# One-hots for the later gathers of a routed-expert layer, made one chunk earlier

## The chip, the cores and the metric

The kernel runs on one core of a Trainium2 chip. The metric is the device time of one execution in microseconds (us), lower is better. In what follows TensorE (PE in the profile) multiplies matrices, with its weight loads shown apart (PEld); VectorE is DVE, ScalarE is ACT, and SyncE (SP) issues every transfer from memory.

## The reference

Two layers of a decoder trunk over 256 tokens of 1024 features in float32: two mixers, a dense feed-forward block, and at the end a routed one. Only that last block is touched:

```python
def moe_swiglu(h, router, w_gate, w_up, w_down):
    t = h.reshape(b * s, d)
    logits = (t @ router).astype(jnp.float32)
    top_val, top_idx = lax.top_k(logits, TOP_K)          # 2 of 8 experts
    top_w = jax.nn.softmax(top_val, axis=-1)
    gates = ...                                          # zero where an expert is not chosen
    out = jnp.zeros_like(t)
    for e in range(N_EXPERTS):
        out = out + gates[:, e:e + 1] * swiglu(t, w_gate[e], w_up[e], w_down[e])
    return out.reshape(b, s, d)
```

Each expert has a gate and an up matrix of 1024 x 2816 and a down matrix of 2816 x 1024.

## The kernel before

The kernel computes for each expert only the rows (tokens) that chose it. The experts are sorted by their number of rows. The four largest ("large", ranks 0 to 3) get 128 rows each and are computed with split weights: every weight is the sum of a rounded part `wh` and a rest `wl`, and three products replace one. The four others ("small") get 64 rows and use the weights as they are. An expert's rows are fetched on TensorE: a one-hot matrix (128 tokens by 128 places, 1 where a token sits in that place) is multiplied with the normalised activations `xnh` and `xnl`. The function `one_hots` makes it on VectorE with one `tensor_tensor` for each half of the tokens, comparing `iota` with the tokens' places `poso`; `gather_all(j, oh, dst)` is the product for the j-th block of 128 features, and ScalarE copies its result into `dst`.

Weights come in units of 1 MB, three to a chunk of 256 hidden features: two for gate and up (`gu0`, `gu1`) and one for down (`dn`). An expert has 11 chunks (FC). Units are loaded in the order of their use into a ring of places (`raw` five times, `xres`, `xg1`, `more`, `fl`, `wx`, `wy`); a place is loaded anew once its unit is split (large) or multiplied (small). The splits run on ScalarE (`wh`) and VectorE (`wl`), two half units each, and are issued by `st.ahead`.

From the first expert's chunk on the order of the work is written out by hand: a list `steps`, and every engine works through its instructions in that order. The large experts' chunks are numbered g = 0 to 43 (expert p, chunk c, g = 11 p + c); the small ones follow LAG = 4 chunks later. From g = 5 on the steps of one g are: transposes of the previous large chunk (`tr`), `gu0`, late scatters, transposes of the small chunk, `dn` of the previous large chunk, `gu1` with the activation and two splits, `rest`, and then the small expert's `dn`, `gu0`, `gu1`.

The step `rest` holds what is not part of the chunk pipeline: the transposed one-hots for the scatters (`oht_of`), and the gathers. At g = 0 to 3 the small experts' rows are gathered, at g = 6 to 9 those of the large experts 1 and 2 together, two blocks of features in each chunk, and at g = 13 to 16 (p = 1, c = 2 to 5) those of expert 3. The one-hots of a group are made at its first gather. They lie in a tile of the ring `tw`, which has 12 buffers and also holds the hidden activations and their transposes.

Of the kernel before, what the change touches and what calls it, by code (L numbers as in the profile page):

```python
# [19 lines left out]
P = 128  # L20
# [35 lines left out]
LAG = 4  # L56
# [338 lines left out]
def kernel(ctx: ExitStack, tc: tile.TileContext, a, out: bass.AP):  # L395
# [29 lines left out]
    def tw(n=512, np_=P, dt=F32):  # L425
        return rec.tile(wkp, [P, 512], dt, "tw", TW, name="tw")[:np_, :n]

    def pa():
        return rec.tile(psp, [P, 512], F32, "ps", 8, name="ps")
# [104 lines left out]
    def bc(ap, shape):  # L534
        return ap.to_broadcast(shape)
# [237 lines left out]
    def ff_gu(st, xs, gu, u, ahead=True):  # L773
        wh, wl = st.next(ahead)
        for b in range(len(xs)):
            for kk in range(4):
                k = 4 * u + kk
                mm3(gu[b], xs[b][0][:, k, :], xs[b][1][:, k, :], wh[:, kk * 512:(kk + 1) * 512],
                    wl[:, kk * 512:(kk + 1) * 512], k == 0, k == 7)

    def ff_act(gu, scales=None, act=None):
        hs = []
        for b in range(len(gu)):
            si = tw(256)
            hh = tw(256)
            if scales:
                tact(si, gu[b][:, 0:256], AF.Silu, scale=scales[b])
                V.scalar_tensor_tensor(hh, gu[b][:, 256:512], scales[b], si, op0=OP.mult, op1=OP.mult)
            else:
                (act or tact)(si, gu[b][:, 0:256], AF.Silu)  # L790
                V.tensor_tensor(hh, gu[b][:, 256:512], si, OP.mult)
            hs.append(hh)
        return hs

    def ff_tr(hs):
        n = 2 * len(hs) * P
        tp = pa()
        transposes([h[:, i * P:(i + 1) * P] for i in range(2) for h in hs], tp)
        th, tl = tw(n, dt=F32R), tw(n, dt=F32R)
        S.activation(th, tp[:, :n], AF.Copy)  # L800
        V.tensor_tensor(tl, tp[:, :n], th.bitcast(F32), OP.subtract)
        return th, tl
# [277 lines left out]
    mo = scope("m")  # L1080
# [389 lines left out]
    def one_hots(lo, n, width=P):  # L1470

        t = tw(2 * n * width, dt=F32R).rearrange("p (b e s) -> p b e s", b=2, e=n)
        for b in range(2):
            V.tensor_tensor(t[:, b], bc(iota[:, None, 0:width], [P, n, width]),
                            bc(poso[:, b, lo:lo + n, None], [P, n, width]), OP.is_equal)
        return t

    def both_halves(r):

        t = tw(256, dt=F32R).rearrange("p (b s) -> p b s", b=2)  # L1480
        for b in range(2):
            V.tensor_scalar(t[:, b].rearrange("p (i s) -> p i s", i=2), bc(iota[:, None, 0:HALFP], [P, 2, HALFP]),
                            poso[:, b, r:r + 1], None, op0=OP.is_equal)
        return t
# [6 lines left out]
    def gather(k, ohs, n):  # L1491

        o = pa()[:, 0:n]
        for i, src in enumerate((xnh, xnl)):
            for b in range(2):
                mmx(o, src[:, b, k * P:(k + 1) * P], ohs(b), i + b == 0, i + b == 2)
        return o, k2("gf1k", k, k + 1)
# [5 lines left out]
    def gather_all(k, oh, dst):  # L1503

        n, w = oh.shape[2], oh.shape[3]
        o, gain = gather(k, lambda b: oh[:, b].rearrange("p e s -> p (e s)"), n * w)
        S.activation(dst[:, :, k], o.rearrange("p (e s) -> p e s", e=n), AF.Copy, scale=gain)
# [8 lines left out]
    def y_split(yps):  # L1516
        rec.late = 0
        y = [(tw(dt=F32R), tw(dt=F32R)) for i in range(2)]
        for i in range(2):
            rec.late = HALF if i else 0  # L1520
            S.activation(y[i][0], yps[i], AF.Copy)
            V.tensor_tensor(y[i][1], yps[i], y[i][0].bitcast(F32), OP.subtract)
        return y

    def scatter(t, y, g, acc, store=False):
        for i in range(2):
            rec.late = HALF if i else 0
            cs = slice(i * 512, (i + 1) * 512)
            for b in range(2):
                sp = pa()  # L1530
                T.matmul(sp, t[:, b * P:(b + 1) * P], y[i][0], start=True, stop=False)
                T.matmul(sp, t[:, b * P:(b + 1) * P], y[i][1], start=False, stop=True)
                V.scalar_tensor_tensor(acc[:, b, cs], sp, g(b), acc[:, b, cs], op0=OP.mult, op1=OP.add)
                if store:
                    dma(ov[:, b, cs], acc[:, b, cs])
        rec.late = 0
# [5 lines left out]
    def large_split(src):  # L1542
        x = large_tile()
        S.activation(x[0], src, AF.Copy)
        V.tensor_tensor(x[1], src, x[0].bitcast(F32), OP.subtract)
        return x


    def sm_gu(xs, gu, u):
        w = st.next(False)  # L1550
        for kk in range(4):
            k = 4 * u + kk
            wv = w[:, kk * 512:(kk + 1) * 512].rearrange("p (g f) -> p g f", g=2)
            for i in range(2):
                mmx(gu[i * HALFP:(i + 1) * HALFP, 0:256].rearrange("p (g f) -> p g f", g=2), xs[:, k],
                    wv[:, :, i * P:(i + 1) * P], k == 0, k == 7)
        st.done()

    def sm_act(gu):
        si, hh = tw(P), tw(P)  # L1560
        tact(si, gu[:, 0:P], AF.Silu)
        V.tensor_tensor(hh, gu[:, P:256], si, OP.mult)
        return hh

    def sm_tr(hh):
        tp = pa()
        transposes([hh], tp)
        t = tw(P)
        S.activation(t, tp[:, 0:P], AF.Copy)
        return t  # L1570

    def sm_dn(t, y, first, last):
        w = st.next(False)
        for hf in range(2):
            for i in range(2):
                mmx(y[hf][i * HALFP:(i + 1) * HALFP, :], t[:, i * HALFP:(i + 1) * HALFP],
                    w[:, i * 1024 + hf * 512:i * 1024 + (hf + 1) * 512], first, last)
        st.done()
# [57 lines left out]
    for n, (k, it) in enumerate(steps):  # L1636
        if k == "late":
            while pend:
                scatter(*pend.pop(0))
            continue  # L1640
        sm, p, c = it
        if k in ("gu0", "gu1"):
            if k == "gu0":
                gu[sm] = pa()
            if sm:
                sm_gu(xs[:, p], gu[sm], unit_of[k])
            else:
                ff_gu(st, [xb], [gu[sm]], unit_of[k], False)
            if k == "gu1":
                hs[sm] = sm_act(gu[sm]) if sm else ff_act([gu[sm]])  # L1650
                if not sm and c == FC - 1 and p < BIG - 1:
                    xb = large_split(xl[:, p % 2])
                if not sm:
                    st.ahead(HL)
                    st.ahead(HL)
                if c == 0:
                    ohs[sm] = n, both_halves(BIG + p) if sm else one_hots(p, 1)[:, :, 0]
        elif k == "tr":
            ts[sm] = sm_tr(hs[sm]) if sm else ff_tr(hs[sm])
            if not sm:  # L1660
                st.ahead(HL)
        elif k == "dn":
            if c == 0:
                ys[sm] = [pa(), pa()]
            if sm:
                sm_dn(ts[sm], ys[sm], c == 0, c == FC - 1)
            else:
                ff_dn(st, ts[sm], [ys[sm]], c == 0, c == FC - 1, False)
            if c == FC - 1:
                r = p + (BIG if sm else 0)  # L1670
                pend.append((ohts[sm], y_split(ys[sm]), lambda b, r=r: gateo[:, b, r:r + 1], x3, n == len(steps) - 2))
        else:
            for e in list(ohs):
                if n >= ohs[e][0] + 5:
                    o = ohs.pop(e)[1]
                    ohts[e] = oht_of(o[:, 0], o[:, 1])
            if p == 0 and c < LAG:
                for j in range(2 * c, 2 * c + 2):
                    gather_all(j, oh_s, xs)
            if p == 0 and LAG + 2 <= c < LAG + 6:  # L1680
                if c == LAG + 2:
                    xl, oh_l = mo([P, 2, 8, P], "xg0"), one_hots(1, 2)
                for j in range(2 * (c - LAG - 2), 2 * (c - LAG - 1)):
                    gather_all(j, oh_l, xl)
            if p == 1 and 2 <= c < 6:
                if c == 2:
                    oh_l = one_hots(3, 1)
                for j in range(2 * c - 4, 2 * c - 2):
                    gather_all(j, oh_l, xl[:, 0:1])
    man.close()  # L1690
# [179 lines left out]
```

## Time and profile before

| | |
|---|---|
| runs | median 1151.38 us (1150.53 to 1153.55, 3 runs) |
| profiled execution | 1152.82 us, span 1151.0 us |
| TensorE busy | 1113.1 us, 97% |
| VectorE busy | 723.1 us, 63% |
| ScalarE busy | 601.4 us, 52% |
| mean granted TensorE clock | 0.985 |
| moved by DMA | 348.15 MB, mean 302 GB/s |

The span runs from the first to the last instruction of the profiled execution; its own time is 1.8 us longer. Busy shares are means over the whole span. Instructions recorded through a helper all carry that helper's line (L333, or L522 to L524 for the three products), so they are told apart by the tiles: `tw<-c,poso` is the making of one-hots, `ps<-tw,xnh` the first product of a gather, `ps<-cp,tw` a transpose, `wl<-raw,wh` half of a split.

### The profile page before, as it was taken

The numbers are of one execution on the slowest core, as the hardware profiler recorded it, in microseconds if no ns is written. First come the engines' busy times: TensorE is split into PE (matmuls) and PEld (weight loads), VectorE is DVE, ScalarE is ACT, GpSimd is POOL, SyncE is SP. The second block draws the span as 40 slices with busy tenths as digits, with TensorE's granted clock in tenths as the row PEclk, the third lists the DMA queues.
The fourth block names the chain that finished last, engine by engine and source line by source line (L and its number), as shares of the span: only waits on it lengthen the run. The fifth ranks groups of instructions, "written<-read, shape, count | busy, mean of one in ns | idle before, by whom it ended". The sixth has DMA issues, their size and how long they took to land.

```text
span 1151.0 us, 16659 instructions
## 1 busy us (share of the span) xinstructions
PE 1113.1 (97%) x6100; PEld 833.5 (72%) x6100; DVE 723.1 (63%) x1325; ACT 601.4 (52%) x1134; POOL 29.1 (3%) x59
## 2 busy tenths in 40 slices
PE   8999999999999999998999799999999999999997
PEld 7887888888787877875676567666666666676653
DVE  6999954544388867785356646556556556565542
ACT  5868644444378656474355435545454554544430
POOL 1050000000300000000000000000000000000000
PEclk9999999999999999899899999999999999999999
DMA  9551555556343633379799989999999999999996
GB/s 345 214 215 37 185 218 188 186 181 218 113 156 124 254 149 147 144 272 382 289 401 408 411 333 390 414 422 422 421 421 420 423 421 422 421 422 422 421 422 248
DMA packets 52216, 348.15 MB, mean 302 GB/s; under 512 B 5920, under 2 KB 6048, under 8 KB 11680
## 3 DMA queue, kind: packets, MB, share of 16 engines
q1 hardware_dynamic: 52128, 347.02, 76.0%
q8 instruction: 50, 0.82, 0.3%
q14 instruction: 38, 0.31, 0.1%
HBM read 345.95 MB, written 1.05 MB: 301 GB/s over the span
## 4 chain that ended last, share of the span: by engine, by line
PE 89%; DMA 5%; DVE 3%; ACT 2%; issue 0%; SPq 0%; DVEq 0%; ACTq 0%
PE ps L333 23%; PE ps L522 19%; PE ps L524 19%; PE ps L523 19%; PE ps L328 10%; DMA raw<-in_moe_dram 3%; DMA more<-in_moe_dram 2%; DVE wl L333 1%; ACT tw L328 1%; DMA raw<-in_w_dram 0%; DVE wl L328 0%; DVE tw L328 0%; ACT wh L333 0%; DVE xres L333 0%; ACT wh L328 0%
## 5 line engine op out<-in xcount | busy, mean ns | idle before, releaser
L333 ACT ACTIVATE tw<-ps 128x256 fp32r<-128x256 f32 (+3 forms) x202 | 72.6, 365 | 360.8 <-PE ps L524 212.5
L522 PE MATMUL ps<-wh,fh 128*128 128x512 f32 (+2 forms) x632 | 254.5, 403 | 0.0
L523 PE MATMUL ps<-wl,fh 128*128 128x512 f32 (+2 forms) x632 | 245.5, 389 | 0.0
L333 DVE TENSOR_TENSOR tw<-ps,tw 128x256 f32<-128x256 f32 (+3 forms) x158 | 64.6, 427 | 264.7 <-ACT tw L333 264.7
L333 DVE TENSOR_TENSOR wl<-raw,wh 128x1024 fp32r<-128x1024 f32 x156 | 183.7, 1224 | 55.9 <-ACT wh L333 55.4
L333 ACT ACTIVATE wh<-raw 128x1024 fp32r<-128x1024 f32 x156 | 155.2, 1050 | 43.7 <-PE ps L524 37.8
L524 PE MATMUL ps<-wh,fh 128*128 128x512 f32 x352 | 138.5, 394 | 0.0
L522 PEld LDWEIGHTS ps<-wh,fh 128*128 128x128 f32 x632 | 119.4, 189 | 22.2 <-issue 0.2
L523 PEld LDWEIGHTS ps<-wl,fh 128*128 128x128 f32 x632 | 119.4, 189 | 21.7 <-issue 0.2
L524 PE MATMUL ps<-wh,fl 128*128 128x512 f32 (+2 forms) x280 | 107.6, 384 | 0.0
L522 PE MATMUL ps<-wh,tw 128*128 128x512 f32 (+1 forms) x252 | 103.2, 410 | 1.8 <-ACT tw L333 1.1
L524 PE MATMUL ps<-wh,tw 128*128 128x512 f32 (+1 forms) x252 | 99.3, 394 | 0.0
L523 PE MATMUL ps<-wl,tw 128*128 128x512 f32 (+1 forms) x252 | 99.2, 394 | 0.0
L333 PE MATMUL ps<-raw,xs 128*64 128x256 f32 x672 | 78.4, 379 | 0.0
L524 PEld LDWEIGHTS ps<-wh,fh 128*128 128x128 f32 x352 | 66.4, 189 | 14.5
L328 DVE TENSOR_TENSOR wl<-raw,wh 128x512 fp32r<-128x512 f32 x113 | 74.7, 680 | 2.9 <-ACT wh L328 2.9
L333 PEld LDWEIGHTS ps<-raw,xs 128*64 128x64 f32 x672 | 47.9, 137 | 33.4 <-issue 11.7
L328 ACT ACTIVATE wh<-raw 128x512 fp32r<-128x512 f32 (+1 forms) x104 | 59.7, 620 | 18.7 <-PE ps L524 11.5
L524 PEld LDWEIGHTS ps<-wh,fl 128*128 128x128 f32 x280 | 52.6, 188 | 10.7 <-DVE fl L328 0.2
L522 PEld LDWEIGHTS ps<-wh,tw 128*128 128x128 f32 x252 | 47.6, 189 | 15.0 <-ACT tw L333 2.2
L524 PEld LDWEIGHTS ps<-wh,tw 128*128 128x128 f32 x252 | 47.4, 188 | 11.4 <-DVE tw L328 0.4
L523 PEld LDWEIGHTS ps<-wl,tw 128*128 128x128 f32 x252 | 47.5, 189 | 9.3
(319 smaller groups left out, 1744.2 us busy)
## 6 DMA issues: line engine op xcount, KB each, us to landing
raw<-in_moe_dram SPq DMA_DIRECT2D x120, 1024.0 KB, 13.9
raw<-in_ffn_dram SPq DMA_DIRECT2D x30, 1024.0 KB, 4.8
xg<-in_moe_dram SPq DMA_DIRECT2D x24, 1024.0 KB, 13.4
more<-in_moe_dram SPq DMA_DIRECT2D x24, 1024.0 KB, 12.9
fl<-in_moe_dram SPq DMA_DIRECT2D x24, 1024.0 KB, 13.2
raw<-in_w_dram SPq DMA_DIRECT2D x23, 1024.0 KB, 4.9
wx<-in_moe_dram SPq DMA_DIRECT2D x23, 1024.0 KB, 14.2
xres<-in_moe_dram SPq DMA_DIRECT2D x23, 1024.0 KB, 14.0
```

The costliest lines, as they stand in the source:

```text
L328: return (self.name, self.cost(fn, args, kw), lambda: real(*args, **kw))
L333: return getattr(self.eng, fn)(*args, **kw)
L522: nc.tensor.matmul(ps, xh, wh, start=start, stop=False)
L523: nc.tensor.matmul(ps, xh, wl, start=False, stop=False)
L524: nc.tensor.matmul(ps, xl, wh, start=False, stop=stop)
```

## The change

The two calls of `one_hots` are moved from the first gather of their group to the `rest` step of the chunk before it: from g = 6 to g = 5 for the large experts 1 and 2, and from g = 13 to g = 12 for expert 3. The tile `xl`, into which the gathers are copied, is still allocated at the first gather.

```diff
             if p == 0 and c < LAG:
                 for j in range(2 * c, 2 * c + 2):
                     gather_all(j, oh_s, xs)
+            if (p, c) in ((0, LAG + 1), (1, 1)):
+                oh_l = one_hots(1, 2) if p == 0 else one_hots(3, 1)
             if p == 0 and LAG + 2 <= c < LAG + 6:
                 if c == LAG + 2:
-                    xl, oh_l = mo([P, 2, 8, P], "xg0"), one_hots(1, 2)
+                    xl = mo([P, 2, 8, P], "xg0")
                 for j in range(2 * (c - LAG - 2), 2 * (c - LAG - 1)):
                     gather_all(j, oh_l, xl)
             if p == 1 and 2 <= c < 6:
-                if c == 2:
-                    oh_l = one_hots(3, 1)
                 for j in range(2 * c - 4, 2 * c - 2):
                     gather_all(j, oh_l, xl[:, 0:1])
```

## Rows read from the trace of the kernel before

**Rows 1.** The page's 40 slices of 28.8 us: granted clock, DMA share, in tenths.
```profile
PEclk9999999999999999899899999999999999999999
DMA  9551555556343633379799989999999999999996
```

**Rows 2.** Windows: length, busy us (instructions) by engine, granted clock, DMA share, GB/s.
```profile
540.00:720.00 180.00, 166.75 (x931) 116.72 (x930) 98.33 (x121) 85.01 (x130) 0.00 (x0) 0.95 0.93 374
720.00:1120.00 400.00, 396.69 (x2224) 272.58 (x2224) 233.89 (x281) 194.26 (x281) 0.00 (x0) 1.00 1.01 421
...
640.00:660.00 20.00, 16.02 (x89) 11.08 (x87) 11.29 (x14) 10.95 (x15) 0.00 (x0) 0.99 1.00 407
```

**Rows 3.** The chain that ended last, in order of time: start, us, what.
```profile
543.64 3.49 DVE wl L333 x3
547.13 0.35 DVE tw L333
...
658.56 3.48 DVE wl L333 x3
...
1051.32 18.05 DMA raw<-in_moe_dram
```

**Rows 4.** Timeline of TensorE: start, us, instruction, idle time before it and its releaser.
```profile
532.26 0.44 PE L333 MATMUL ps<-cp,tw 128*128 128x128 f32 x2
...
535.29 0.27 PE L333 MATMUL ps<-cp,tw 128*128 128x128 f32 x1
...
547.62 0.82 PE L333 MATMUL ps<-tw,xnh 128*128 128x256 f32 x2 [6.51 <-DVE tw L333]
...
557.03 0.44 PE L333 MATMUL ps<-cp,tw 128*128 128x128 f32 x2
...
572.09 0.44 PE L333 MATMUL ps<-cp,tw 128*128 128x128 f32 x2
...
647.18 0.44 PE L333 MATMUL ps<-cp,tw 128*128 128x128 f32 x2
...
650.21 0.27 PE L333 MATMUL ps<-cp,tw 128*128 128x128 f32 x1
...
662.40 0.66 PE L333 MATMUL ps<-tw,xnh 128*128 128x128 f32 x2 [6.37 <-DVE tw L333]
...
670.67 0.44 PE L333 MATMUL ps<-cp,tw 128*128 128x128 f32 x2
...
685.60 0.44 PE L333 MATMUL ps<-cp,tw 128*128 128x128 f32 x2
```

**Rows 5.** Timeline of VectorE around the two places, same columns.
```profile
532.74 0.42 DVE L333 CAST tw<-ps 128x256 fp32r<-128x256 f32 x1
533.07 0.61 DVE L333 TENSOR_TENSOR tw<-ps,tw 128x128 f32<-128x128 f32 x2
534.10 2.36 DVE L333 TENSOR_TENSOR wl<-wy,wh 128x1024 fp32r<-128x1024 f32 x2 [0.41 <-ACT wh L333]
...
542.50 4.63 DVE L333 TENSOR_TENSOR wl<-raw,wh 128x1024 fp32r<-128x1024 f32 x4 [0.52 <-ACT wh L333]
547.05 0.75 DVE L333 TENSOR_TENSOR tw<-c,poso 128x256 fp32r<-128x256 f32 x2
...
647.99 0.61 DVE L333 TENSOR_TENSOR tw<-ps,tw 128x128 f32<-128x128 f32 x2
...
661.97 0.48 DVE L333 TENSOR_TENSOR tw<-c,poso 128x128 fp32r<-128x128 f32 x2
```

**Rows 6.** Windows behind the two places, columns as in rows 2.
```profile
547.60:557.00 9.40, 9.38 (x48) 5.13 (x48) 0.20 (x1) 0.95 (x2) 0.00 (x0) 0.67 0.80 303
557.00:572.10 15.10, 15.10 (x90) 10.81 (x88) 8.13 (x9) 7.73 (x12) 0.00 (x0) 1.00 0.67 247
...
662.40:670.70 8.30, 8.30 (x49) 4.80 (x49) 0.05 (x1) 0.73 (x2) 0.00 (x0) 0.75 0.97 393
670.70:685.60 14.90, 14.90 (x89) 10.72 (x88) 8.14 (x9) 7.52 (x12) 0.00 (x0) 1.00 0.74 268
```

**Rows 7.** Waits of TensorE from 530 us on: total us, times, longest.
```profile
PE ps L333 <- DVE tw L333: 15.6, 6, 6.5
```

## The prediction

> **What bounds the kernel now.** I read the page first, for the slices of the clock and of the DMA engines [rows 1]. The reader is to see three things: the clock's digit is 8 in the 17th slice, which lies before the change, and in the 20th, which holds its first half; the DMA digit is 7 in that 20th slice too; and it is 9 from the 21st to the last but one, save for an 8 in the 24th. So where TensorE's clock dips, the transfers slacken. Next the windows, which turn the digits into rates [rows 2]: from 720 to 1120 us the DMA engines are full at 421 GB/s; from 540 to 720 they move 374 GB/s on average. Then the chain of waits [rows 3]: it runs along TensorE, but steps off it at 543 and at 658 us, through three weight splits on VectorE and then (at 547.13) the one-hot tile; and from 1051 us on it is made of single transfers of 18 us and more. So the last 100 us are set by the transfers, the rest by TensorE, and a change has to move both to move the end. The timeline of TensorE then shows the two places, and that of VectorE what it was doing there [rows 4, 5].
>
> The two places are the first gather of a group: at chunk 6 of expert 0 (g = 6) and at chunk 2 of expert 1 (g = 13). TensorE stops at 541 us and starts again at 547.62 after 6.51 us idle; the second time it starts at 662.40 after 6.37 us idle [rows 4]. VectorE makes the one-hots only at 547.05 and 661.97, behind the four half-unit splits of that chunk, 4.63 us the first time [rows 5]. The wait costs more than itself: TensorE resumes at the lower of its two clock levels, 1.2 GHz instead of 2.4. The granted clock is 0.67 on average from 547.6 to 557.0 and 0.75 from 662.4 to 670.7, with 1.00 in the stretches after them [rows 6].
>
> **The change part by part.** *The two waits.* The whole price, idle and slow clock together, is read from chunk lengths between the transposes that open each chunk [rows 4]. Chunk g = 6 lasts 557.03 - 532.26 = 24.77 us; g = 7, with the same gathers, 572.09 - 557.03 = 15.06. Loss 9.71. Chunk g = 13 lasts 670.67 - 647.18 = 23.49; g = 14, with the same gathers, 685.60 - 670.67 = 14.93. Loss 8.56. Sum 18.27 us of TensorE. All waits of TensorE for a `tw` tile of VectorE from 530 us on are 15.6 us in 6 cases [rows 7], and these two are 12.88 of it; the rest is at the end of the kernel and not touched.
>
> With the one-hots made a chunk earlier, the gather's operands are old when TensorE reaches it. What comes next is not late: after the gather follow small products on units that landed long before, and then the transposes of a hidden tile that VectorE finishes before the splits.
>
> *The moved instructions.* Nothing is added or removed: two tensor_tensor of 0.75 us together for experts 1 and 2, and two of 0.48 us for expert 3 (the second pair begins at 661.97 and is the 128-column form) [rows 5]. No DMA moves. The copy of the gathered rows stays where it is. They now stand on VectorE in the rest step of the chunk before, behind the transposed one-hots' copy (the CAST at 532.74) and in front of the two products that the next transposes and the next down product read. At g = 6 these end at 533.07 + 0.61 = 533.68; with 0.75 more at 534.43, and TensorE wants them at 535.29: 0.86 us to spare. The split behind them would come 0.75 us later too, and has a whole down product before TensorE asks for it. At g = 13 they would end at 647.99 + 0.61 + 0.48 = 649.08 and are wanted at 650.21: 1.13 to spare [rows 4, 5]. So I cost the move at nothing; without that cover it is 0.75 + 0.48 = 1.23 us, as the upper end. A gain from it I exclude, since VectorE idles in both chunks anyway.
>
> *The buffer.* `oh_l` occupies one of twelve `tw` buffers for a chunk longer. Before the change the same tile is already held through four chunks, and the one after the stalled one runs at its 15.06 us [rows 4]. Cost between nothing and, should VectorE wait for a buffer, the rival below.
>
> *What the transfers allow.* The end is set by transfers, so TensorE's 18.27 us count only as far as the transfers come earlier too. Slots come free as TensorE and the splits use up units, so both holes are followed by a slack in the DMA engines: share 0.80 and 0.67 after the first, 0.97 and 0.74 after the second [rows 6]. Counting only that missing share: 0.20 x 9.4 + 0.33 x 15.1 + 0.03 x 8.3 + 0.26 x 14.9 = 11.0 us. Counting bytes: 180 us at 374 GB/s would take 159.9 us at 421, the rate seen when the queue is never empty, which saves 20.1; at the 407 GB/s of 640 to 660 us, a full share just after the queue was shallow, they take 165.4 and save 14.6 [rows 2]. TensorE caps the gain at 18.3. Between 14.6 and 18.3 I take 17.4, three quarters of the way, since with the holes gone the queue is nearer to its state after 720 us, where 421 is held for 400 us, than to that at 640 us.
>
> From 720 us on nothing changes but the origin of time, since TensorE and transfers have moved by about the same; the lead of the transfers is used up near the end as before.
>
> The sum is made against the profiled execution: 1152.8 us, span 1151.0. The median of the runs is 1151.4, 1.4 lower, and I take the saving off it: 1151.4 - 17.4 = 1134.0. A measurement of this kernel tells a change from none at about 0.3%, 3.5 us.
>
> **The rivals.**
>
> *The transfers give only their idle share (B).* If the engines at share 1.00 can't go faster than they did before 720 us, only the 11.0 us of missing share come back: 1140.4. For it: the chain's end is made of transfers [rows 3]. Against it: the same engines hold 421 GB/s later with the same units. The Trainium skill, Perfetto Trace Analysis, in the section on identifying the most-contended engine, has one optimise the engine that is fullest first and judges DMA by its throughput; its note on the roofline puts a single core's 16 DMA engines at about 435 GB/s. By that rule TensorE's stalls beside nearly full DMA engines are worth only the room left in those engines, which is this rival. The trace agrees for the stretch after 720 us, where it is full at 421, and not for 540 to 720 us at 374.
>
> *Only one hole closes (C).* The first gather may find another wait in the place of one of them: a PSUM buffer, or a unit that hasn't landed now that TensorE comes 9.7 us earlier. Then 8.6 or 9.7 us come back: 1141.7 to 1142.8. For it: the DMA engines were not ahead at will after the holes. Against it: the gathers of g = 7 and g = 14 stand in the same place of their chunk, take the same buffers in turn, and have no such loss.
>
> *Nothing moves (D).* The one-hots could still reach VectorE late, or the transfers could set every stage: 1151.4. Against it: VectorE passes the new place at 533 and 648 us, 8 and 8 us before the gathers are due, and the DMA engines do idle.
>
> *Slower (E).* In its new place the one-hot holds up an in-order VectorE. If it had to wait for a `tw` buffer that is freed only by work of the following chunk, the products behind it would be late by up to a chunk, and TensorE would stop at the transposes instead. Only what exceeds the 0.86 and 1.13 us of cover counts; the kernel loses on balance from 18.3 + 3.5 = 21.8 us together, 11 at each place. A full chunk at each would be 15.06 + 14.93 - 1.99 - 18.27 = 9.7 us more: 1161.1. Against it: at that place VectorE has just copied a tile that TensorE made after all the chunk's earlier reads, so that the buffers read before are free.
>
> **How the numbers follow.** Forecast (both holes gone, 1133.1 to 1136.8): 0.70. B 0.15, C 0.08, D 0.04, E 0.03. A, B and C are faster by over 0.3%: 0.93; D is the same, 0.04; E slower, 0.03. The range reaches from 1131.5 (the 20.1 us that the bytes would allow: 1131.3) to 1141, which takes in B and leaves out C, D and E, 0.15.
>
> **What would show it.** Right: no idle time before the products on `tw,xnh` at g = 6 and g = 13; chunks of about 15.1 and 14.9 us there; the clock at 1.00 through both; one-hots on VectorE about 8 us before they are read; a DMA share of 1.00 from some 560 us on, and the same slow drift into waits for transfers in the last 60 us. Wrong: a wait of TensorE at the transposes at the chunk's start (E); a DMA rate that stays near 400 GB/s with the share at 1.00 (B); an idle row with another releaser at either gather (C); TensorE gaining 18 us by 720 us and idling them away before the end.

## The result and the profile after

| | before | after |
|---|---|---|
| median of 6 runs each, same chip | 1152.34 us | 1133.59 us |
| lowest to highest | 1150.53 to 1153.55 | 1131.77 to 1134.25 |
| span of the profiled execution | 1151.0 us | 1132.5 us |
| mean granted TensorE clock | 0.985 | 0.993 |

The ratio is 0.9836, 95% interval 0.9824 to 0.9849: the change makes the kernel 18.75 us faster by the medians, 17.4 to 20.3 by the interval. The forecast was 1134.0 us, in a range of 1131.5 to 1141.0.

The 40 slices of the page (28.3 us each), which answer to [rows 1]:

```profile
PEclk9999999999999999899999999999999999999999
DMA  9551465556334634278999999999999999999996
```

The digit 8 of the clock in the 20th slice is gone; the one in the 17th lies before the change and stays. The DMA digits are 9 from the 20th slice to the last but one, without the dips of before.

The timeline of TensorE, for [rows 4]: start, us, instruction, idle time before it.

```profile
531.34 0.44 PE L333 MATMUL ps<-cp,tw 128*128 128x128 f32 x2
...
534.37 0.27 PE L333 MATMUL ps<-cp,tw 128*128 128x128 f32 x1
...
540.01 0.40 PE L333 MATMUL ps<-tw,xnh 128*128 128x256 f32 x2
...
546.37 0.44 PE L333 MATMUL ps<-cp,tw 128*128 128x128 f32 x2
...
636.52 0.44 PE L333 MATMUL ps<-cp,tw 128*128 128x128 f32 x2
...
639.55 0.27 PE L333 MATMUL ps<-cp,tw 128*128 128x128 f32 x1
...
645.20 0.33 PE L333 MATMUL ps<-tw,xnh 128*128 128x128 f32 x2
...
651.46 0.44 PE L333 MATMUL ps<-cp,tw 128*128 128x128 f32 x2
```

The first products of the gathers, at 540.01 and 645.20, have no idle time before them, and run in 0.40 and 0.33 instead of 0.82 and 0.66 us. Chunk g = 6 lasts 546.37 - 531.34 = 15.03 us and g = 13 lasts 651.46 - 636.52 = 14.94; before they lasted 24.77 and 23.49 [rows 4]. TensorE gains 9.74 + 8.55 = 18.29 us there. (Chunk g = 6 also begins 0.92 us earlier than in the profile of before. That lies ahead of the change; in the profiles of the experiments below the same chunk begins between 529.98 and 532.33 us.)

The timeline of VectorE, for [rows 5]:

```profile
531.81 0.42 DVE L333 CAST tw<-ps 128x256 fp32r<-128x256 f32 x1
532.15 0.75 DVE L333 TENSOR_TENSOR tw<-c,poso 128x256 fp32r<-128x256 f32 x2
532.82 0.61 DVE L333 TENSOR_TENSOR tw<-ps,tw 128x128 f32<-128x128 f32 x2
...
637.33 0.48 DVE L333 TENSOR_TENSOR tw<-c,poso 128x128 fp32r<-128x128 f32 x2
637.74 0.61 DVE L333 TENSOR_TENSOR tw<-ps,tw 128x128 f32<-128x128 f32 x2
```

The one-hots stand where they were expected, between the CAST and the two products. These end at 533.43 and TensorE takes them at 534.37, 0.94 us later; at g = 12 and 13 they end at 638.35 and are taken at 639.55, 1.20 us later. So the move is covered.

The windows of the stretches that answer to [rows 2] and [rows 6] (length, busy us by engine, clock, DMA share, GB/s), shifted by 18 us where they lie behind both holes:

```profile
546.40:561.50 15.10, 15.10 (x90) 10.84 (x89) 8.13 (x9) 7.73 (x12) 0.00 (x0) 1.00 1.01 421
651.50:666.40 14.90, 14.90 (x90) 10.72 (x88) 8.14 (x9) 7.52 (x12) 0.00 (x0) 1.00 1.01 422
...
540.00:702.00 162.00, 161.63 (x933) 114.67 (x932) 98.87 (x120) 85.10 (x131) 0.00 (x0) 1.00 1.00 415
702.00:1102.00 400.00, 396.02 (x2220) 271.79 (x2220) 232.92 (x281) 193.40 (x279) 0.00 (x0) 1.00 1.01 422
```

The chunks after the two places, in which the transfers fell to 247 and 268 GB/s, now see 421 and 422. From 540 to 702 us the rate is 415 GB/s against 374 before.

The chain that ended last, for [rows 3], near its end:

```profile
961.24 20.52 DMA fl<-in_moe_dram
981.87 19.87 DMA raw<-in_moe_dram
...
1033.17 18.03 DMA raw<-in_moe_dram
1051.32 19.73 DMA raw<-in_moe_dram
1071.17 19.70 DMA more<-in_moe_dram
```

The last three transfers stand where the three of before did: they begin at 1033.17 us instead of 1051.32, 18.15 us earlier. The chain now also runs over two transfers from 961.24 us on, where that of before was still on TensorE, so the transfers set the end over a longer stretch than they did.

### The profile page after: what moved, and what is told of

It reads as the page before. It is cut to its first block, busy times and chain, and to the rows that moved or that the text cites. A ratio compares the mean times of both kernels' runs of the same rounds, so it can differ in the third digit from the quotient of the medians.

```text
span 1132.5 us, 16661 instructions
## 1 busy us (share of the span) xinstructions
PE 1107.4 (98%) x6100; PEld 829.8 (73%) x6100; DVE 723.0 (64%) x1325; ACT 600.4 (53%) x1134; POOL 28.9 (3%) x59
## 4 chain that ended last, share of the span: by engine, by line
PE 86%; DMA 9%; DVE 2%; ACT 2%; issue 1%; SPq 0%; DVEq 0%; ACTq 0%
PE ps L333 21%; PE ps L522 18%; PE ps L524 18%; PE ps L523 18%; PE ps L328 10%; DMA raw<-in_moe_dram 5%; DMA fl<-in_moe_dram 2%; DMA more<-in_moe_dram 2%; ACT tw L328 1%; DVE wl L333 1%; DMA raw<-in_xT_dram 0%; DVE wl L328 0%; DVE tw L328 0%; ACT wh L333 0%; SPq L443 0%
## 5 line engine op out<-in xcount | busy, mean ns | idle before, releaser
L524 PEld LDWEIGHTS ps<-wh,fh 128*128 128x128 f32 x352 | 66.6, 189 | 14.6
L328 ACT ACTIVATE wh<-raw 128x512 fp32r<-128x512 f32 (+1 forms) x104 | 59.7, 619 | 17.8 <-PE ps L524 11.5
```

The lines of the kernel that those rows point to most:

```text
L328: return (self.name, self.cost(fn, args, kw), lambda: real(*args, **kw))
L524: nc.tensor.matmul(ps, xl, wh, start=False, stop=stop)
```

## The experiments

Each ran beside the kernel before on the same chip. The theory is that of the prediction: each hole has a price of its own, idle time plus slow clock, set by the place of the one-hots behind the splits; the transfers follow TensorE in full, and then set the end. The rivals are named with each run.

**One half at a time.** The two places are moved separately.

```diff
-            if (p, c) in ((0, LAG + 1), (1, 1)):
-                oh_l = one_hots(1, 2) if p == 0 else one_hots(3, 1)
+            if (p, c) == (0, LAG + 1):
+                oh_l = one_hots(1, 2)
...
             if p == 1 and 2 <= c < 6:
+                if c == 2:
+                    oh_l = one_hots(3, 1)
```

> Only the one-hots of experts 1 and 2 are made a chunk early; those of expert 3 stay at their first gather. Theory (each hole has its own price, 9.7 us here, and the transfers follow TensorE in full): 9.7 us less than before, 1142.6 us; chunk g = 6 at 15.05 us, chunk g = 13 still at 23.5 us with its idle time of 6.4 us. Rival (the transfers give back only their idle share, 0.20 x 9.4 + 0.33 x 15.1): 6.9 us less, 1145.4. Rival (the holes are one late queue: closing the first one lengthens or closes the second): chunk g = 13 differs from 23.5 by more than 1 us.

Measured: 1142.60 us, ratio 0.9928 (0.9911 to 0.9944), 9.5 us less by the medians and 6.4 to 10.3 by the interval.

The other half keeps `one_hots(1, 2)` at g = 6 and moves `one_hots(3, 1)` to `(1, 1)`:

```diff
+            if (p, c) == (1, 1):
+                oh_l = one_hots(3, 1)
...
-                    xl = mo([P, 2, 8, P], "xg0")
+                    xl, oh_l = mo([P, 2, 8, P], "xg0"), one_hots(1, 2)
```

> Only the one-hots of expert 3 are made a chunk early. Theory: 8.6 us less than before, 1143.7 us; chunk g = 6 still at 24.8 us, chunk g = 13 at 14.9 us; with the other half alone the two savings add up to the whole. Rival (transfers give only their idle share, 0.03 x 8.3 + 0.26 x 14.9): 4.1 us less, 1148.2.

Measured: 1143.93 us, ratio 0.9935 (0.9918 to 0.9951), 8.2 us less by the medians and 5.6 to 9.4 by the interval.

The timeline of TensorE with the first half alone, around the second place:

```profile
635.53 0.44 PE L333 MATMUL ps<-cp,tw 128*128 128x128 f32 x2
...
650.75 0.66 PE L333 MATMUL ps<-tw,xnh 128*128 128x128 f32 x2 [6.38 <-DVE tw L333]
...
659.28 0.44 PE L333 MATMUL ps<-cp,tw 128*128 128x128 f32 x2
```

The second hole is untouched: 6.38 us idle, chunk 659.28 - 635.53 = 23.75 us, against 6.37 and 23.49 before. The first, whose one-hots were moved, is gone: chunk g = 6 takes 15.03 us. With the second half alone the first hole is idle for 6.51 us as before (row below, under what was not expected), and chunk g = 13 takes 14.93 us. So the holes are not one late queue. The savings 9.5 and 8.2 add up to 17.7 of 18.75 us, which agrees within their intervals. The rival that only the idle share of the transfers comes back, 6.9 and 4.1 us, falls with the second: 4.1 lies outside 5.6 to 9.4. For the first alone, 6.9 lies inside 6.4 to 10.3 and is not excluded by its run.

**The place within the chunk.** Both groups stay in the chunk of their first gather, once between the activation's product and the splits, once ahead of the activation.

```diff
                 hs[sm] = sm_act(gu[sm]) if sm else ff_act([gu[sm]])
+                if not sm and (p, c) in ((0, LAG + 2), (1, 2)):
+                    oh_l = one_hots(1, 2) if p == 0 else one_hots(3, 1)
...
-            if (p, c) in ((0, LAG + 1), (1, 1)):
-                oh_l = one_hots(1, 2) if p == 0 else one_hots(3, 1)
```

> Both groups of one-hots stay in the chunk of their first gather, but stand on VectorE between the activation's product and the four half splits. Theory (the price is the place behind the splits): TensorE waits only for the activation's product and the one-hots, some 1.7 us at g = 6 and 1.4 us at g = 13, and its clock stays at 1.00; 18.7 less 3.1 is 15.6 us less than before, 1136.7 us. Rival (any wait lowers the clock, 3.2 and 2.2 us more): 1142. Rival (a chunk's distance is needed): 1152.

Measured: 1136.38 us, ratio 0.9872 (0.9856 to 0.9889). TensorE, at the first place and at the second:

```profile
530.08 0.44 PE L333 MATMUL ps<-cp,tw 128*128 128x128 f32 x2
...
540.28 0.63 PE L333 MATMUL ps<-tw,xnh 128*128 128x256 f32 x2 [1.36 <-DVE tw L333]
...
546.87 0.44 PE L333 MATMUL ps<-cp,tw 128*128 128x128 f32 x2
...
647.08 0.43 PE L333 MATMUL ps<-tw,xnh 128*128 128x128 f32 x2 [1.23 <-DVE tw L333]
```

The waits are 1.36 and 1.23 us, and chunk g = 6 takes 546.87 - 530.08 = 16.79 us. The granted clock stays at full speed:

```profile
530.00:560.00 30.00, 28.64 (x160) 20.55 (x160) 15.87 (x21) 14.81 (x23) 0.00 (x0) 1.00 0.99 407
```

So a wait of 1.36 us costs only itself and some start-up (16.79 - 15.03 = 1.76 us), where one of 6.51 costs 9.7 (8.4 in one other execution, last section).

The second variant has the same two lines ahead of the activation's line.

> Both groups of one-hots in the chunk of their first gather, on VectorE ahead of the activation's product, where VectorE idles for 5 us. Theory: no wait at all, as with the change, 1133.6 us; chunks g = 6 and g = 13 at 15.05 and 14.93. Rival (a chunk's distance is needed, or the one-hots delay the activation and so the transposes): idle time of TensorE at either place, above 1136.

Measured: 1133.23 us, ratio 0.9841 (0.9825 to 0.9858), no idle time at either gather; the first, and the one-hots that VectorE makes in its idle time within the chunk:

```profile
539.14 0.40 PE L333 MATMUL ps<-tw,xnh 128*128 128x256 f32 x2
```

```profile
534.58 0.76 DVE L333 TENSOR_TENSOR tw<-c,poso 128x256 fp32r<-128x256 f32 x2
539.75 0.42 DVE L333 TENSOR_TENSOR tw<-ps,tw 128x256 f32<-128x256 f32 x1 [4.42 <-ACT tw L333]
540.70 4.63 DVE L333 TENSOR_TENSOR wl<-raw,wh 128x1024 fp32r<-128x1024 f32 x4 [0.52 <-ACT wh L333]
```

This equals the change within the measurement. What counts is that the one-hots stand ahead of the activation's product, for which VectorE itself waits (4.42 us here), and so ahead of the splits too; a whole chunk's distance is not needed. Ahead of the splits alone, as in the variant before, left the waits of 1.36 and 1.23 us.

**The cover.** Each group is written four times over.

```diff
             if (p, c) in ((0, LAG + 1), (1, 1)):
                 oh_l = one_hots(1, 2) if p == 0 else one_hots(3, 1)
+                for i in range(3):
+                    n = 2 if p == 0 else 1
+                    lo = 1 if p == 0 else 3
+                    for b in range(2):
+                        V.tensor_tensor(oh_l[:, b], bc(iota[:, None, 0:P], [P, n, P]),
+                                        bc(poso[:, b, lo:lo + n, None], [P, n, P]), OP.is_equal)
```

> As with the change, but each group of one-hots is written four times over into the same tile, so that VectorE spends 2.25 us more at g = 5 and 1.44 us more at g = 12. Theory (the move is hidden by 0.94 and 1.20 us of cover, read from the trace of the change): TensorE waits some 1.3 us at the transposes of g = 6 and 0.2 us at those of g = 13, and since the transfers are full from 545 us on, the time rises by no more than that: 1133.6 to 1135.2 us. Rival (the place is not on TensorE's path at all): no wait in the trace, 1133.6. Rival (the wait also lowers the clock): 1138 and more.

Measured: 1133.62 us, ratio 0.9851 (0.9835 to 0.9866), as with the change. VectorE, and then TensorE at the transposes of g = 6:

```profile
530.79 2.76 DVE L333 TENSOR_TENSOR tw<-c,poso 128x256 fp32r<-128x256 f32 x8
533.47 0.61 DVE L333 TENSOR_TENSOR tw<-ps,tw 128x128 f32<-128x128 f32 x2
```

```profile
529.98 0.44 PE L333 MATMUL ps<-cp,tw 128*128 128x128 f32 x2
...
533.81 0.33 PE L333 MATMUL ps<-cp,tw 128*128 128x128 f32 x1 [0.64 <-DVE tw L333]
...
545.87 0.44 PE L333 MATMUL ps<-cp,tw 128*128 128x128 f32 x2
```

The wait comes where it was expected, 0.64 us long; chunk g = 6 takes 15.89 us, 0.86 more than with the change, and g = 13 takes no more. I had expected 1.3 and 0.2: eight one-hots in a row take 2.76 us, not 4 x 0.75 = 3.0, and the transposes begin at 533.81, before the two products behind the one-hots end at 533.47 + 0.61 = 534.08, while I had counted to the end of both. The lost 0.86 us do not show in the time, but a difference of that size is below what these runs resolve.

**The slow clock alone.** The kernel before, with products that nobody reads in the holes.

```diff
+            if (p, c) in ((0, LAG + 2), (1, 2)):
+                idle2 = pa()
+                for i in range(26 if p == 0 else 25):
+                    mmx(idle2, xnh[:, 0, 0:P], xnh[:, 1, 0:512], True, True)
             if p == 0 and LAG + 2 <= c < LAG + 6:
```

> The kernel before, with 26 and 25 products of 128x512 that nobody reads put on TensorE ahead of the two first gathers, some 6.0 and 5.8 us at full clock, which end before the one-hots are there. Theory (part of each hole is the slow clock behind it): the idle time turns into work, the clock stays at 1.00, chunks g = 6 and g = 13 fall to 15.05 + 6.5 = 21.6 and 14.93 + 6.4 = 21.3; 5.4 us less than before, 1146.9 us. Rival (the slow clock costs nothing, since the transfers are behind anyway): 1152.3.

Measured: 1148.02 us, ratio 0.9962 (0.9951 to 0.9974). TensorE and, below, the windows of its two chunks:

```profile
532.03 0.44 PE L333 MATMUL ps<-cp,tw 128*128 128x128 f32 x2
...
540.71 6.10 PE L333 MATMUL ps<-xnh 128*128 128x512 f32 x26
547.39 0.63 PE L333 MATMUL ps<-tw,xnh 128*128 128x256 f32 x2 [0.58 <-DVE tw L333]
...
553.98 0.44 PE L333 MATMUL ps<-cp,tw 128*128 128x128 f32 x2
```

```profile
532.10:554.00 21.90, 21.32 (x115) 15.63 (x114) 9.44 (x13) 7.96 (x12) 0.00 (x0) 1.00 0.99 400
...
646.00:668.00 22.00, 21.33 (x115) 15.75 (x114) 8.95 (x12) 8.16 (x13) 0.00 (x0) 1.00 1.01 417
```

The gather starts no earlier than in the kernel before (547.39), yet the chunk ends 3 us sooner: 553.98 - 532.03 = 21.95 us instead of 24.77, and 21.58 instead of 23.49 at g = 13, some 0.3 us above the 21.6 and 21.3 expected. The two clock losses are 2.82 and 1.91 us, 4.73 together, of which the time shows 4.3 (3.0 to 5.6 by the interval). That is about a quarter of the 18.27 us, and the two waits, 12.88 us, are most of the rest. The first loss is taken against one execution: against the 23.46 us that the same chunk took in another (last section) it is 1.51 us, and the two together are 3.42, which the interval holds too.

**What sets the end now.** The change without the gathers for expert 3.

```diff
-            if (p, c) in ((0, LAG + 1), (1, 1)):
+            if (p, c) in ((0, LAG + 1),):
...
-            if p == 1 and 2 <= c < 6:
+            if False:
```

> As with the change, but without the eight gathers for expert 3 and their one-hots (expert 3 is computed on the rows of expert 1): TensorE has 4 x 0.85 = 3.4 us less to do at g = 13 to 16. Theory (from 545 us on the transfers run at 414 to 422 GB/s and set the end): no more than 1 us less than with the change, 1132.6 to 1133.6, and TensorE idles the rest away later. Rival (TensorE sets the end): 1130.2 us.

Measured: 1134.04 us (1132.04 to 1134.77), ratio 0.9839 (0.9826 to 0.9851): no gain over the change, and within the spread of these runs no different from the 1132.6 to 1133.6 expected. The windows, and then TensorE at the transposes that open g = 13 and g = 14, and at two later ones:

```profile
540.00:702.00 162.00, 161.63 (x916) 113.33 (x915) 98.44 (x118) 83.08 (x123) 0.00 (x0) 1.00 1.00 416
702.00:1102.00 400.00, 394.81 (x2210) 269.52 (x2210) 232.44 (x280) 194.15 (x279) 0.00 (x0) 1.00 1.01 422
```

```profile
637.51 0.44 PE L333 MATMUL ps<-cp,tw 128*128 128x128 f32 x2
...
651.60 0.44 PE L333 MATMUL ps<-cp,tw 128*128 128x128 f32 x2
...
724.14 0.44 PE L333 MATMUL ps<-cp,tw 128*128 128x128 f32 x2
...
1075.94 0.44 PE L333 MATMUL ps<-cp,tw 128*128 128x128 f32 x2
```

Chunk g = 13 takes 651.60 - 637.51 = 14.09 us instead of 14.94, so TensorE did save its time there, some 0.84 us in each of four chunks. The transfers move at the rates of the change, 416 and 422 GB/s. From the two holes on they set the end, and 3.4 us less of TensorE's work are worth nothing that shows. TensorE gives them back: with the change the transposes that begin here at 724.14 begin at 726.51, so the lead is 2.37 us there, and those at 1075.94 begin at 1076.05, a lead of 0.11 us. The chain that ended last runs over a transfer from 857.49 us on in this run, 104 us earlier than with the change.

## Why the prediction was right

- *The two waits, 18.27 us of TensorE.* Right in size and place: 18.29 us by the chunks after, and each half alone gives its part.
- *The slow clock as part of the price.* Right. It was taken from chunk lengths without being split; filled holes split it, 4.73 of 18.27 us.
- *The move at no cost.* Right: 0.94 and 1.20 us to spare, where 0.86 and 1.13 were forecast. With four times the work the cover is gone at the first place, as it should be, and the wait is 0.64 us.
- *The buffer.* No wait of VectorE for it shows; rival E did not occur.
- *The transfers.* Here the size was off. I took three quarters of the way from 14.6 to 18.3, 17.4 us; measured are 18.75 (17.4 to 20.3), so that by the medians the transfers follow TensorE in full; 17.4 is the lower end of the interval. Their rate from 540 to 702 us is 415 GB/s, between the 407 and the 421 of the two bounds. By the same arithmetic 180 x 374 / 415 = 162.2 us, 17.8 saved; with the 0.92 us by which chunk g = 6 begins earlier in this profile it is 18.7, against 18.5 between the two spans.
- *The number.* The forecast of 1134.0 us came within 0.4 us of the measured 1133.59, closer than its parts, and that is luck: the prediction started from 1151.4 us for the kernel before, which over six runs measured 1152.34, and took off 1.35 us too little, so two differences of about 1 us cancel.
- *Rival B* (11.0 us) fails: the engines at share 1.00 did move faster once the queue was never empty. The prediction tied it to the rule of the Trainium skill, in Perfetto Trace Analysis, section on identifying the most-contended engine, to optimise the most contended engine first, which would be the DMA engines. The trace agrees with that order for the kernel after (no gain from less work on TensorE), and not for the kernel before, where the stalls of TensorE were followed by the fall of the transfers to 247 and 268 GB/s. The price of 11.0 us, only the room left in the DMA engines, was the prediction's own reading of the rule, and it is this reading that the runs refute.
- *Rivals C and D* did not occur. No other wait took the place of the two.
- *The distance of a whole chunk is not needed.* The same time comes from one-hots in the same chunk, ahead of the activation.

## What to carry to other kernels

On an engine that works in order, a small operation that another engine waits for must stand ahead of bulk work that nobody waits for yet, and ahead of that engine's own long waits; a place in the idle time before the activation did as much as a chunk's distance, a place just behind it left waits of 1.36 and 1.23 us. A stall on the engine that frees the buffers costs the transfers later, so read the DMA rate in the stretch behind a stall before calling the transfers the limit. And price a stall by the length of the whole stage against its neighbour, since the idle time alone (12.9 us here) left out 5.4 us of slow clock and start-up.

## What the runs showed that was not expected

The same idle time did not always cost the same. With only the second half moved, the first hole is idle for 6.51 us, as before:

```profile
530.34 0.44 PE L333 MATMUL ps<-cp,tw 128*128 128x128 f32 x2
...
545.69 0.82 PE L333 MATMUL ps<-tw,xnh 128*128 128x256 f32 x2 [6.51 <-DVE tw L333]
...
553.80 0.44 PE L333 MATMUL ps<-cp,tw 128*128 128x128 f32 x2
```

Its chunk takes 553.80 - 530.34 = 23.46 us, not 24.77. The window from the restart to the end of the chunk (columns as above) has a mean clock of 0.78, against 0.67 in the kernel before:

```profile
545.70:553.80 8.10, 8.10 (x48) 4.72 (x48) 0.18 (x1) 0.95 (x2) 0.00 (x0) 0.78 0.88 336
```

So the clock came back to the upper level sooner after the restart in that execution. Why is not shown by these runs.

Shorter waits did not all spare the clock either. Those of 1.36 and 1.23 us left it at its upper level. But in the profile of the filled holes TensorE waits 2.80 us near the end, and the window behind that wait is at the lower level, 0.50:

```profile
1109.44 0.33 PE L333 MATMUL ps<-cp,tw 128*128 128x128 f32 x1 [2.80 <-DVE tw L333]
```

```profile
1110.00:1112.00 2.00, 2.00 (x7) 1.52 (x6) 0.00 (x0) 0.09 (x1) 0.00 (x0) 0.50 1.00 418
```

And in the kernel before, ahead of the change, two waits of only 1.08 and 1.16 us, which end at 460.52 and 462.37 us with four small products between them, are followed by 8 us at the lower level, the dip of the 17th slice:

```profile
462.00:470.00 8.00, 7.63 (x34) 7.57 (x35) 5.47 (x25) 2.83 (x8) 0.00 (x0) 0.50 0.17 36
```

So the length of a single wait doesn't tell whether the clock falls, and where it begins to fall stays open.
